# Chunk scan of a hybrid decoder step: the state product in three passes of rounded parts, and x times d on GpSimd

## The chip, the cores and the metric

The kernel runs on one core of one Trainium2 chip. A core has five engines that work at the same time, each through its own list of instructions in order: PE (TensorE, matrix products into PSUM; its weight loads, PEld, are listed apart), DVE (VectorE), ACT (ScalarE), POOL (GpSimd) and SP, which issues DMAs. An engine waits at an instruction until what it needs (data, or a buffer that is free) is there, and everything behind it waits too. The metric is the time of one execution in microseconds; a lower one is better. What is compared is the median of several executions.

## The reference

One step of a hybrid decoder layer for 512 prompt positions and 8 single new tokens (520 columns in all), model width 1024: an FFN of width 2816, a mixer, a second FFN, a final norm. The mixer adds causal pooling over windows of 2 to 16 and a Mamba-2 scan with 16 heads of 64 and a state of 128. The scan, cut to what matters:

```
xc, dtc, Bc, Cc = chunks of 128 positions; 16 heads in 2 groups of 8
Acs    = cumsum(dtc * A) within a chunk
scores = C . B                       for two positions l, s of a chunk
y_diag = sum_s scores * exp(Acs_l - Acs_s), s <= l, * dt_s * x_s
states = sum_s B_s * exp(Acs_end - Acs_s) * dt_s * x_s
h      = exp(Acs_end) * h + states   from chunk to chunk
y_off  = C_l . h * exp(Acs_l)
y      = y_diag + y_off + d_skip * x
```

All is fp32, and the kernel keeps fp32's accuracy in its products.

## The kernel before

Activations lie with their features on the 128 partitions and the 520 columns along them, in two halves of 260. A large product isn't done on fp32 operands: each operand is split in a rounded part (type fp32r, "hi", cast by ACT) and the rest ("lo", a subtraction by DVE), and three passes add hi x hi, hi x lo and lo x hi in one PSUM bank (`mm3`, lines 150 to 155, and `mm_low_last`, L157 to L165, which names the passes L160 and L165). Small products of the scan stay fp32.

The mixer is written as plans, strings of stages that are issued one after the other: the input projection's parts (x, b, z), pooling (p, c, m), the samples (s, r), the output projection (o, g, h), and for the scan A0 to A7 and B0 to B7. Stage j stands for chunk c = j mod 4 and group g = j div 4, so that a pair is named "cg": 00, 10, 20, 30, then 01, 11, 21, 31. `ssd_a` prepares a pair: PE transposes B (pb) and x (px), ACT copies B's transpose to bt, DVE masks the scores (scm) and scales x by dt (xdt), a DMA brings the sums of the decay (ab), ACT and DVE turn them into a decay matrix in place (G is ab), GpSimd makes xw (xdt times the decay to the chunk's end, we), and DVE multiplies ab by scm (L1247). `ssd_b` does the products: yo (the state hst against C, 4 matmuls of 128 columns, from chunk 1 on), pst (bt against xw, the new state's share, one matmul of 512 columns), yd (xdt against ab, 8 matmuls), then the update of hst (GpSimd multiplies by the chunk's decay cd, DVE adds pst), and on DVE E times yo, plus yd, and last X = X times d_skip + E, four operations of 128 columns with a scalar per partition (L1276). X is where x lies and where y is left; E holds exp of the sums, and the next pair's E may start once a buffer is free.

The order in which each engine gets its instructions isn't the order of the plans alone: the framework's scheduler, which places instructions by its own estimate of their times as far as the dependences allow, merges the stages of the plans, so that an edit moves work elsewhere. The banks of PSUM are 8, used in turn: a product waits until the bank that it gets has been read. xw has two buffers; ab, bt and scm have three; X is one tile.

In the names below, inx, inz and inp are banks of the input projection for x, z and pooling (the digits give the block of 128 rows and the half), zs the place to which DVE evacuates inz (L1284), PW and PU the tiles of pooling, A the accumulator of the convolution (L1025, L1027), h_60 and cb60 a sample's state and its B and C, which come back by a DMA from DRAM (L1144), catp and tlo parts of the output projection.

Of the kernel before, what the change touches and what calls it, by code (L numbers as in the profile page):

```python
# [10 lines left out]
F32 = mybir.dt.float32  # L11
F32R = mybir.dt.float32r
AF = mybir.ActivationFunctionType
ALU = mybir.AluOpType
# [3 lines left out]
P = 128  # L18
# [11 lines left out]
CH = 128  # L30
# [28 lines left out]
VEC = {}  # L59
# [838 lines left out]
def mixer(tc, ins, outs, e):  # L898
    nc = tc.nc
    cst, act, wp, tmp, dr, pool = (e[x] for x in ("cst", "act", "wp", "tmp", "dr", "pool"))  # L900
    ones, queued, squared = e["ones"], e["queued"], tuple(e["added"])
    bank, load_unit, mm3, mm_low_last, ws, v, rstd, rstds, vec, h, nx2, raw_tile, open_f2, fin, fill = (
        e[x] for x in ("bank", "load_unit", "mm3", "mm_low_last", "ws", "v", "rstd", "rstds", "vec", "h", "nx2", "raw_tile",
                       "open_f2", "fin", "fill"))
    xh, xl, _, r = nx2[0]
    xa = e["xa"][0]
    mp = pool("mx", "right")
# [16 lines left out]
    X = mp.tile([P, NX, NT], F32, tag="X", name="X")  # L924
# [279 lines left out]
    pair = {}  # L1204

    def ssd_a(c, g):
        cs = slice(c * CH, (c + 1) * CH)
        pb = bank(f"pb{c}{g}")
        nc.tensor.transpose(pb[:, :P], BC[:, g, cs], ident)
        nc.tensor.matmul(pb[:, P : 2 * P], BC[:, g, cs], BC[:, 2 + g, cs], start=True, stop=True)  # L1210
        bt = mp.tile([P, P], F32, tag="bt", bufs=3, name=f"bt{c}{g}")
        nc.scalar.copy(bt, pb[:, :P])
        scm = mp.tile([P, P], F32, tag="scm", bufs=3, name=f"scm{c}{g}")
        nc.vector.tensor_tensor(out=scm, in0=pb[:, P : 2 * P], in1=tri, op=ALU.mult)
        px = bank(f"px{c}{g}")
        for q in range(4):
            nc.tensor.transpose(px[:, q * P : (q + 1) * P], X[:, 4 * g + q, cs], ident)
        ab = mp.tile([P, 8, P], F32, tag="ab", bufs=3, name=f"ab{c}{g}")
        nc.sync.dma_start(out=ab, in_=scr_acs[c * NH + 8 * g : c * NH + 8 * g + 8].unsqueeze(0).to_broadcast([P, 8, P]))
        dtc = tok[:, 0, c, 8 * g : 8 * g + 8]  # L1220
        atc = tok[:, 1, c, 8 * g : 8 * g + 8]
        we = mp.tile([P, 8], F32, tag="we", bufs=2, name=f"we{c}{g}")
        nc.gpsimd.tensor_tensor(out=we, in0=ab[:, :, CH - 1], in1=atc, op=ALU.subtract)
        nc.scalar.activation(out=we, in_=we, func=AF.Exp)
        E = cd = None
        if c > 0:
            E = mp.tile([P, 4, P], F32, tag="E", bufs=2, name=f"E{c}{g}")
            for j in range(2):
                nc.scalar.activation(out=E[64 * j : 64 * j + 64], in_=ab[64 * j : 64 * j + 64, j::2, :], func=AF.Exp)
            cd = mp.tile([P, 8], F32, tag="cd", bufs=2, name=f"cd{c}{g}")  # L1230
            nc.scalar.activation(out=cd, in_=ab[:, :, CH - 1], func=AF.Exp)
        G = ab
        for q in range(ON_ACT):
            nc.scalar.activation(out=G[:, q], in_=ab[:, q], func=AF.Relu, scale=-1.0, bias=atc[:, q : q + 1])
        for q in range(ON_ACT, 8):
            nc.vector.tensor_scalar(out=G[:, q], in0=ab[:, q], scalar1=atc[:, q : q + 1], scalar2=0.0,
                                    op0=ALU.subtract, op1=ALU.min)
        with queued(*(held["silu"] if (c, g) == (3, 0) else ())):
            nc.scalar.activation(out=G[:, :ON_ACT], in_=G[:, :ON_ACT], func=AF.Exp, scale=-1.0)
            held["exp"] = nc.scalar.activation(out=G[:, ON_ACT:], in_=G[:, ON_ACT:], func=AF.Exp)  # L1240
        xdt = mp.tile([P, 8, 64], F32, tag="xdt", bufs=2, name=f"xdt{c}{g}")
        nc.vector.tensor_tensor(out=xdt, in0=px.rearrange("p (a b) -> p a b", a=8),
                                in1=dtc.unsqueeze(2).to_broadcast([P, 8, 64]), op=ALU.mult)
        xw = mp.tile([P, 8, 64], F32, tag="xw", bufs=2, name=f"xw{c}{g}")
        nc.gpsimd.tensor_tensor(out=xw, in0=xdt, in1=we.unsqueeze(2).to_broadcast([P, 8, 64]), op=ALU.mult)
        with queued(*(held["catp"] if (c, g) == (0, 0) else ())):
            nc.vector.tensor_tensor(out=G, in0=G, in1=scm.unsqueeze(1).to_broadcast([P, 8, P]), op=ALU.mult)  # L1247
        pair[c, g] = bt, xdt, xw, G, E, cd

    def ssd_b(c, g):  # L1250
        cs = slice(c * CH, (c + 1) * CH)
        bt, xdt, xw, G, E, cd = pair[c, g]
        if c > 0:
            yo = bank(f"yo{c}{g}")
            for q in range(4):
                nc.tensor.matmul(yo[:, q * P : (q + 1) * P], hst[:, g, q * P : (q + 1) * P], BC[:, 2 + g, cs],
                                 start=True, stop=True)
        pst = bank(f"pst{c}{g}")
        nc.tensor.matmul(pst, bt, xw.rearrange("p a b -> p (a b)"), start=True, stop=True)
        yd = bank(f"yd{c}{g}")  # L1260
        for q in range(8):
            nc.tensor.matmul(yd[64 * (q % 2) : 64 * (q % 2) + 64, (q // 2) * P : (q // 2 + 1) * P], xdt[:, q],
                             G[:, q], start=True, stop=True)
        if c == 0:
            nc.scalar.copy(hst[:, g], pst)
        else:
            hv8 = hst[:, g].rearrange("p (a b) -> p a b", a=8)
            nc.gpsimd.tensor_tensor(out=hv8, in0=hv8, in1=cd.unsqueeze(2).to_broadcast([P, 8, 64]), op=ALU.mult)
            nc.vector.tensor_tensor(out=hst[:, g], in0=pst, in1=hst[:, g], op=ALU.add)
        yr = yd.rearrange("p (q l) -> p q l", q=4)  # L1270
        if c > 0:
            nc.vector.tensor_tensor(out=E, in0=yo.rearrange("p (q l) -> p q l", q=4), in1=E, op=ALU.mult)
            nc.vector.tensor_tensor(out=E, in0=yr, in1=E, op=ALU.add)
            yr = E
        for q in range(4):
            nc.vector.scalar_tensor_tensor(out=X[:, 4 * g + q, cs], in0=X[:, 4 * g + q, cs],  # L1276
                                           scalar=v("d_skip", 4 * g + q), in1=yr[:, q], op0=ALU.mult, op1=ALU.add)

    def zproj(j):
        if not zbox:  # L1280
# [75 lines left out]
    def outs_a():  # L1356
# [16 lines left out]
        "s": samples,  # L1373
        "r": lambda n: samples(n, True),
        "A": lambda j: ssd_a(*ssd(j)),
        "B": lambda j: ssd_b(*ssd(j)),
        "z": zproj,
        "o": lambda j: wout(catp, 0, j),
# [107 lines left out]
```

## Time and profile before

| what | us |
|---|---|
| median of 3 runs (lowest, highest) | 954.37 (954.22, 955.53) |
| span of the profiled execution | 951.9 |
| PE busy | 942.5 |
| PEld (weight loads, beside PE) | 925.9 |
| DVE busy | 852.7 |
| ACT busy | 635.7 |
| POOL busy | 148.3 |

The profiled execution is known by its span, from its first instruction to its last; the time of a run has some 2.5 us more around that, by the median. The scan of the chunks lies between about 410 and 560 us. A row of a group gives the line, the engine, the operation, out<-in by the program's names, the count, and the shortest, median and longest duration in ns; a row of the timeline gives the start, the time until the group's end, the engine and the line, and in brackets how long the engine had been idle before it and for whom. Matmuls and DVE instructions overlap with the next of their queue by a little, so the time from start to start is what one costs in a row of them.

### The profile page before, as it was taken

Reading aid. Unit: us, or ns where it says so; the run is one execution under the profiler, and the core shown is the slowest. Engines: PE = TensorE matmul, PEld = TensorE weight load, DVE = VectorE, ACT = ScalarE, POOL = GpSimd, SP = SyncE. Lnnn points to the kernel's source line nnn. Section 1 sums busy time; section 2 is a strip of 40 time slices with the busy share of each in tenths; the row PEclk is TensorE's granted clock in tenths of the full one; section 3 lists DMA queues with packets and bytes.
Section 4 is the critical chain, followed back from the end, with each engine's and each line's share of the span. In section 5 each row is a group of like instructions: output and inputs, shape, how many; then the busy total and the mean of one; then the engine's idle time right before and its main releaser. Section 6 shows DMA issues by size and latency. Waiting matters only on the chain.

```text
span 951.9 us, 19681 instructions
## 1 busy us (share of the span) xinstructions
PE 942.5 (99%) x7674; PEld 925.9 (97%) x7674; DVE 852.7 (90%) x1462; ACT 635.7 (67%) x1179; POOL 148.3 (16%) x230
## 2 busy tenths in 40 slices
PE   9999999999999999999999999999999999999996
PEld 8999999999999999999999999999999999999996
DVE  6899899998988688789998998999999999999886
ACT  7777756677566455485668735777776676766774
POOL 0011100100100000046251100111112101122120
PEclk9999999999999999999999999999999999999998
DMA  7666554455553343354264453556666655776552
GB/s 205 187 166 150 143 151 135 115 140 156 134 155 95 86 134 122 92 180 138 91 184 133 141 114 115 138 122 160 163 173 176 163 146 144 171 194 185 145 180 91
DMA packets 53995, 138.35 MB, mean 145 GB/s; under 512 B 7750, under 2 KB 15878, under 8 KB 53902
## 3 DMA queue, kind: packets, MB, share of 16 engines
q1 hardware_dynamic: 39918, 104.19, 34.2%
q0 software_dynamic: 13712, 32.78, 18.7%
q8 instruction: 60, 0.98, 0.4%
q14 instruction: 33, 0.27, 0.1%
q10 hardware_dynamic: 272, 0.13, 0.0%
HBM read 129.74 MB, written 7.34 MB: 144 GB/s over the span
## 4 chain that ended last, share of the span: by engine, by line
PE 44%; DVE 2%; issue 1%; POOL 1%; DMA 1%; ACT 1%; DVEq 0%; ACTq 0%; POOLq 0%
PE A L160 8%; PE BE L160 6%; PE wo L160 5%; PE A L165 4%; PE BE L165 3%; PE wo L165 2%; PE P L311 1%; PE dh L155 1%; PE dh L151 1%; PE dh L154 1%; POOL zs L1068 1%; PE inz L151 1%; PE inz L154 1%; PE inz L155 1%; DMA room<-in_state_ssm 1%
## 5 line engine op out<-in xcount | busy, mean ns | idle before, releaser
L504 ACT COPY ac<-A 128x260 f32<-128x260 f32 x85 | 31.6, 372 | 35.4 <-PE A L155 17.3
L433 DVE TENSOR_TENSOR s<-raw 128x1024 f32<-128x1024 f32 x39 | 47.6, 1222 | 4.4 <-DMA raw<-in_w2gu 2.8
L504 ACT COPY ac<-BE 128x260 f32<-128x260 f32 x41 | 15.4, 376 | 33.6 <-PE BE L165 17.7
L151 PE MATMUL inx<-xh_mx,whi_inx 128*128 128x260 f32 x112 | 31.8, 284 | 0.0
L154 PE MATMUL inx<-xl_mx,whi_inx 128*128 128x260 f32 x112 | 31.6, 282 | 0.0
L155 PE MATMUL inx<-xh_mx,wlo_inx 128*128 128x260 f32 x112 | 31.6, 282 | 0.0
L1027 DVE SCALAR_TENSOR_TENSOR A<-U,h,A 128x544 f32<-128x544 f32 x36 | 29.0, 807 | 1.6 <-ACT A L1025 1.2
L311 PE MATMUL P<-x,raw 128*128 128x260 f32 x128 | 28.9, 385 | 0.2 <-DMA raw<-in_w1gu 0.2
L311 PEld LDWEIGHTS P<-x,raw 128*128 128x128 f32 x128 | 24.4, 192 | 4.2 <-DMA raw<-in_w1gu 0.6
L160 PE MATMUL wo<-catg,whi_wo 128*128 128x260 f32 x192 | 27.4, 285 | 0.0
L1193 ACT ACTIVATE so<-br,sxdt 128x128 f32<-128x128 f32 x64 | 22.8, 376 | 5.8 <-DVE room L1195 5.2
L160 PEld LDWEIGHTS wo<-catg,whi_wo 128*128 128x128 f32 x192 | 24.8, 188 | 0.2
L139 ACT CAST thi<-raw 128x1024 fp32r<-128x1024 f32 (+1 forms) x14 | 14.2, 1012 | 15.7 <-PE wo L160 4.8
L1304 DVE TENSOR_TENSOR h<-wo,h 128x260 f32<-128x260 f32 x48 | 19.2, 422 | 5.0 <-PE wo L165 4.7
L252 DVE TENSOR_TENSOR gs<-gq,gs 128x780 fp32r<-128x780 f32 (+1 forms) x28 | 23.3, 831 | 0.0
L151 PE MATMUL inz<-xh_mx,whi_inz 128*128 128x260 f32 x80 | 23.0, 287 | 0.0
L154 PE MATMUL inz<-xl_mx,whi_inz 128*128 128x260 f32 x80 | 22.7, 284 | 0.0
L155 PE MATMUL inz<-xh_mx,wlo_inz 128*128 128x260 f32 x80 | 22.6, 283 | 0.0
L251 ACT CAST gs<-gq 128x780 fp32r<-128x780 f32 (+1 forms) x28 | 20.6, 735 | 1.2 <-DVE gq L555 0.8
L151 PEld LDWEIGHTS inx<-xh_mx,whi_inx 128*128 128x128 f32 x112 | 21.1, 188 | 0.2 <-issue 0.2
L160 PE MATMUL A<-xth_f,qs 128*128 128x260 f32 x84 | 21.2, 283 | 0.0
L160 PE MATMUL A<-xtl_f,qs 128*128 128x260 f32 x84 | 21.2, 284 | 0.0
(3140 smaller groups left out, 4382.9 us busy)
## 6 DMA issues: line engine op xcount, KB each, us to landing
raw<-in_w2gu SPq DMA_DIRECT2D x44, 512.0 KB, 4.4
raw<-in_w1gu SPq DMA_DIRECT2D x41, 512.0 KB, 4.3
raw<-in_w_in SPq DMA_DIRECT2D x24, 512.0 KB, 3.7
raw<-in_w1d SPq DMA_DIRECT2D x16, 512.0 KB, 4.6
raw<-in_w2d SPq DMA_DIRECT2D x16, 512.0 KB, 4.6
raw<-in_w_out SPq DMA_DIRECT2D x12, 512.0 KB, 3.5
ab<-scr_acs SPq DMA_DIRECT2D x8, 512.0 KB, 5.5
h<-in_state_ssm SPq DMA_DIRECT2D x16, 256.0 KB, 3.7
```

Of the source, the lines that this page charges most:

```text
L151: first = nc.tensor.matmul(ps, whi, xhi, start=start, stop=False, **kw)
L154: nc.tensor.matmul(ps, whi, xlo, start=False, stop=False, **kw)
L155: nc.tensor.matmul(ps, wlo, xhi, start=False, stop=stop, **kw)
L160: mm = nc.tensor.matmul(ps, w, x, start=start, stop=False, **kw)
L165: nc.tensor.matmul(ps, w, xhi[k], start=False, stop=k == len(wlo) - 1, **kw)
L251: cast = nc.scalar.copy(hi, s)
L252: low = nc.vector.tensor_tensor(out=lo, in0=s, in1=hi.bitcast(F32), op=ALU.subtract)
L311: mm = nc.tensor.matmul(self.banks[f, u][b][:, :HB], ws(self.raw[f][:, u], j + 4 * q), xg[:, slot[q]], start=j == q == 0, stop=j == 3 and ...
L433: nc.vector.tensor_tensor(out=s1, in0=diag, in1=up0, op=ALU.add)
L504: self.copied = nc.scalar.copy(keep, out[:, :HB]).ins
L1027: nc.vector.scalar_tensor_tensor(out=A[:, :n], in0=U[:, j : j + n], scalar=w(j), in1=A[:, :n], op0=ALU.mult, op1=ALU.add)
L1193: nc.scalar.activation(out=o[:, q], in_=br, func=AF.Copy, scale=sxdt[:, j, b : b + 1]))
```

## The change

The state product pst isn't a matmul of fp32 operands any more. ACT rounds B's transpose to bt (fp32r, as a copy with a cast) and DVE makes the rest, btl; xw is split in xwh (ACT) and xwl (DVE); pst is `mm3` over them, three passes of 512 columns, and it is issued after yd, where it stood before yd. xw itself is made at the start of `ssd_b` instead of in `ssd_a`, by GpSimd as before; xw, xwh and xwl have one buffer each. And X = X times d + E is taken apart: GpSimd multiplies X by d_skip in place, 4 x 128 columns in one instruction, in `ssd_a` behind xdt; DVE adds E (for chunk 0, yd) to it in one instruction of 512 columns in place of four.

```diff
@@ -1208,8 +1208,9 @@
         pb = bank(f"pb{c}{g}")
         nc.tensor.transpose(pb[:, :P], BC[:, g, cs], ident)
         nc.tensor.matmul(pb[:, P : 2 * P], BC[:, g, cs], BC[:, 2 + g, cs], start=True, stop=True)
-        bt = mp.tile([P, P], F32, tag="bt", bufs=3, name=f"bt{c}{g}")
-        nc.scalar.copy(bt, pb[:, :P])
+        bt = tuple(mp.tile([P, P], F32R, tag=t, bufs=n, name=f"{t}{c}{g}") for t, n in (("bt", 3), ("btl", 2)))
+        nc.scalar.copy(bt[0], pb[:, :P])
+        nc.vector.tensor_tensor(out=bt[1], in0=pb[:, :P], in1=bt[0].bitcast(F32), op=ALU.subtract)
         scm = mp.tile([P, P], F32, tag="scm", bufs=3, name=f"scm{c}{g}")
         nc.vector.tensor_tensor(out=scm, in0=pb[:, P : 2 * P], in1=tri, op=ALU.mult)
         px = bank(f"px{c}{g}")
@@ -1241,26 +1242,33 @@
         xdt = mp.tile([P, 8, 64], F32, tag="xdt", bufs=2, name=f"xdt{c}{g}")
         nc.vector.tensor_tensor(out=xdt, in0=px.rearrange("p (a b) -> p a b", a=8),
                                 in1=dtc.unsqueeze(2).to_broadcast([P, 8, 64]), op=ALU.mult)
-        xw = mp.tile([P, 8, 64], F32, tag="xw", bufs=2, name=f"xw{c}{g}")
-        nc.gpsimd.tensor_tensor(out=xw, in0=xdt, in1=we.unsqueeze(2).to_broadcast([P, 8, 64]), op=ALU.mult)
+        skip = vec[:, VEC["d_skip"] + 4 * g : VEC["d_skip"] + 4 * g + 4].unsqueeze(2).to_broadcast([P, 4, CH])
+        xs = X[:, 4 * g : 4 * g + 4, cs]
+        nc.gpsimd.tensor_tensor(out=xs, in0=xs, in1=skip, op=ALU.mult)
         with queued(*(held["catp"] if (c, g) == (0, 0) else ())):
             nc.vector.tensor_tensor(out=G, in0=G, in1=scm.unsqueeze(1).to_broadcast([P, 8, P]), op=ALU.mult)
-        pair[c, g] = bt, xdt, xw, G, E, cd
+        pair[c, g] = bt, xdt, we, G, E, cd
 
     def ssd_b(c, g):
         cs = slice(c * CH, (c + 1) * CH)
-        bt, xdt, xw, G, E, cd = pair[c, g]
+        bt, xdt, we, G, E, cd = pair[c, g]
+        xw = mp.tile([P, 8, 64], F32, tag="xw", name=f"xw{c}{g}")
+        nc.gpsimd.tensor_tensor(out=xw, in0=xdt, in1=we.unsqueeze(2).to_broadcast([P, 8, 64]), op=ALU.mult)
+        xwh, xwl = (mp.tile([P, 512], F32R, tag=t, name=f"{t}{c}{g}") for t in ("xwh", "xwl"))
+        xw = xw.rearrange("p a b -> p (a b)")
+        nc.scalar.copy(xwh, xw)
+        nc.vector.tensor_tensor(out=xwl, in0=xw, in1=xwh.bitcast(F32), op=ALU.subtract)
         if c > 0:
             yo = bank(f"yo{c}{g}")
             for q in range(4):
                 nc.tensor.matmul(yo[:, q * P : (q + 1) * P], hst[:, g, q * P : (q + 1) * P], BC[:, 2 + g, cs],
                                  start=True, stop=True)
-        pst = bank(f"pst{c}{g}")
-        nc.tensor.matmul(pst, bt, xw.rearrange("p a b -> p (a b)"), start=True, stop=True)
         yd = bank(f"yd{c}{g}")
         for q in range(8):
             nc.tensor.matmul(yd[64 * (q % 2) : 64 * (q % 2) + 64, (q // 2) * P : (q // 2 + 1) * P], xdt[:, q],
                              G[:, q], start=True, stop=True)
+        pst = bank(f"pst{c}{g}")
+        mm3(pst, *bt, xwh, xwl, True, True)
         if c == 0:
             nc.scalar.copy(hst[:, g], pst)
         else:
@@ -1272,9 +1280,8 @@
             nc.vector.tensor_tensor(out=E, in0=yo.rearrange("p (q l) -> p q l", q=4), in1=E, op=ALU.mult)
             nc.vector.tensor_tensor(out=E, in0=yr, in1=E, op=ALU.add)
             yr = E
-        for q in range(4):
-            nc.vector.scalar_tensor_tensor(out=X[:, 4 * g + q, cs], in0=X[:, 4 * g + q, cs],
-                                           scalar=v("d_skip", 4 * g + q), in1=yr[:, q], op0=ALU.mult, op1=ALU.add)
+        xs = X[:, 4 * g : 4 * g + 4, cs]
+        nc.vector.tensor_tensor(out=xs, in0=yr, in1=xs, op=ALU.add)
 
     def zproj(j):
         if not zbox:
```

The order of the instructions changes with it. Three places follow. First DVE around the decay matrix of pair 30 (its product with the mask is the row `ab30<-ab30,scm30`); E20 and xdt01 belong to the pairs 20 and 01, zs<-inz10 evacuates a bank of z, sxdt belongs to the samples. Before:

```order
L1284 TENSOR_TENSOR zs_5724<-inz01_5729,r_mx_3921 128x260
L1273 TENSOR_TENSOR E20_5556<-yd20_5787,E20_5556 128x512
L1247 TENSOR_TENSOR ab30_5695<-ab30_5695,scm30_5688 128x1024
L1214 TENSOR_TENSOR scm01_5809<-pb01_5804,tri_4294 128x128
L1242 TENSOR_TENSOR xdt01_5831<-px01_5811,tok_4361 128x512
L1276 SCALAR_TENSOR_TENSOR X_4306<-X_4306,h_69,E20_5556 128x128 x4
L1284 TENSOR_TENSOR zs_5724<-inz10_5841,r_mx_3921 128x260
L1247 TENSOR_TENSOR ab01_5816<-ab01_5816,scm01_5809 128x1024
```

After:

```order
L1281 TENSOR_TENSOR E20_5565<-yd20_5805,E20_5565 128x512
L1260 TENSOR_TENSOR xwl30_5916<-xw30_5913,xwh30_5915 128x512
L1213 TENSOR_TENSOR btl01_5827<-pb01_5823,bt01_5826 128x128
L1215 TENSOR_TENSOR scm01_5830<-pb01_5823,tri_4294 128x128
L1135 TENSOR_TENSOR sxdt_4369<-sdt_4367,X_4306 128x32
L1291 TENSOR_TENSOR zs_5738<-inz00_5742,r_mx_3921 128x260
L1291 TENSOR_TENSOR zs_5738<-inz01_5743,r_mx_3921 128x260
L1284 TENSOR_TENSOR X_4306<-E20_5565,X_4306 128x4x128
L1291 TENSOR_TENSOR zs_5738<-inz10_5861,r_mx_3921 128x260
L1249 TENSOR_TENSOR ab30_5710<-ab30_5710,scm30_5703 128x1024
L1249 TENSOR_TENSOR ab01_5837<-ab01_5837,scm01_5830 128x1024
```

The product for ab30 stood right behind yd20's addition; now xwl30, btl01, scm01, three evacuations of z and the addition to X of pair 20 stand between, and xdt01 comes after it.

Second, pair 10: PE's products, and GpSimd ahead of them. PE before:

```order
L1217 MATMUL px20_5546<-ident_4292,X_4306 128x128 x4
L1256 MATMUL yo10_5576<-BC_4307,hst_4374 128x128 x4
L1259 MATMUL pst10_5581<-xw10_5460,bt10_5429 128x512
L1262 MATMUL yd10_5583<-ab10_5438,xdt10_5458 64x128 x8
L151 MATMUL inx70_5605<-xh_mx_3918,whi_inx7_5601 128x260
L154 MATMUL inx70_5605<-xl_mx_3919,whi_inx7_5601 128x260
```

PE after:

```order
L1218 MATMUL px20_5555<-ident_4292,X_4306 128x128 x4
L1264 MATMUL yo10_5590<-BC_4307,hst_4374 128x128 x4
L1268 MATMUL yd10_5595<-ab10_5446,xdt10_5466 64x128 x8
L151 MATMUL pst10_5604<-xwh10_5586,bt10_5435 128x512
L151 MATMUL inx70_5618<-xh_mx_3918,whi_inx7_5614 128x260
L154 MATMUL inx70_5618<-xl_mx_3919,whi_inx7_5614 128x260
L155 MATMUL inx70_5618<-xh_mx_3918,wlo_inx7_5615 128x260
L154 MATMUL pst10_5604<-xwl10_5587,bt10_5435 128x512
L155 MATMUL pst10_5604<-xwh10_5586,btl10_5436 128x512
```

yd10 stands ahead of pst10, and three passes of the projection inx70 stand between the first pass of pst10 and the other two. GpSimd, where PW2 and PU2 are pooling's, before:

```order
L1068 TENSOR_TENSOR PW2_1_5404<-PU2_5398 128x654
L1075 COPY spool_4302<-PU2_5398 128x120
L1068 TENSOR_TENSOR PW2_2_5406<-PW2_1_5404 128x652
L1245 TENSOR_TENSOR xw10_5460<-xdt10_5458,we10_5440 128x512
L1068 TENSOR_TENSOR PW2_4_5408<-PW2_2_5406 128x648
```

GpSimd after (the row with X is pair 10's multiplication by d_skip; d_skip lies in h's tile):

```order
L1068 TENSOR_TENSOR PW2_1_5410<-PU2_5404 128x654
L1075 COPY spool_4302<-PU2_5404 128x120
L1247 TENSOR_TENSOR X_4306<-X_4306,h_69 128x4x128
L1068 TENSOR_TENSOR PW2_2_5412<-PW2_1_5410 128x652
L1256 TENSOR_TENSOR xw10_5584<-xdt10_5466,we10_5448 128x512
L1068 TENSOR_TENSOR PW2_4_5414<-PW2_2_5412 128x648
```

The multiplication of X by d is put between the copy of pooling's state and the second sum of pooling, and xw10 now stands behind both.

Third, DVE where z is evacuated beside the samples (h_50 to h_70 are samples' states). Before:

```order
L1144 TENSOR_TENSOR h0_40_6182<-h0_40_6182,cb40_6180 128x512
L1144 TENSOR_TENSOR h0_50_6191<-h0_50_6191,cb50_6189 128x512
L1284 TENSOR_TENSOR zs_5724<-inz40_6221,r_mx_3921 128x260
L1144 TENSOR_TENSOR h0_60_6200<-h0_60_6200,cb60_6198 128x512
L1284 TENSOR_TENSOR zs_5724<-inz41_6222,r_mx_3921 128x260
L1144 TENSOR_TENSOR h0_70_6209<-h0_70_6209,cb70_6207 128x512
L141 TENSOR_TENSOR wlo_inz7_6568<-raw_74,whi_inz7_6567 128x1024
```

After:

```order
L1144 TENSOR_TENSOR h0_50_6222<-h0_50_6222,cb50_6220 128x512
L1291 TENSOR_TENSOR zs_5738<-inz40_6252,r_mx_3921 128x260
L1260 TENSOR_TENSOR xwl11_6319<-xw11_6316,xwh11_6318 128x512
L1291 TENSOR_TENSOR zs_5738<-inz41_6253,r_mx_3921 128x260
L1144 TENSOR_TENSOR h0_60_6231<-h0_60_6231,cb60_6229 128x512
L1144 TENSOR_TENSOR h0_70_6240<-h0_70_6240,cb70_6238 128x512
L141 TENSOR_TENSOR wlo_inz7_6606<-raw_74,whi_inz7_6605 128x1024
```

The evacuation of inz41 and the subtraction xwl11 stand ahead of the sample's product with cb60; the evacuation stood behind it.

## The prediction

> **What bounds the kernel.** I read the page's busy times first, then the busy times by stretches of 10 us through the mixer, then the chain of waits there, the groups of the tiles that the change touches, and the timeline at the places where TensorE (PE) comes close to waiting. The first lines say what the kernel is made of:
>
> ```profile
> span 951.9 us, 19681 instructions
> PE 942.5 (99%) x7674; PEld 925.9 (97%) x7674; DVE 852.7 (90%) x1462; ACT 635.7 (67%) x1179; POOL 148.3 (16%) x230
> ```
>
> PE is busy for 99% of the span, so time is won only by shorter work on PE or by removing a wait of PE, and lost by any new wait. The median of the runs, 954.37, lies 2.5 us above this span; I make the sum on the trace and add it to the median. About 0.2% (1.9 us) is what a measurement of this kernel can tell from no change: faster is below 952.46, slower above 956.28.
>
> The stretches that hold the chunk scan:
>
> ```profile
> 440.00:450.00 10.00, 10.00 (x88) 9.07 (x87) 9.55 (x17) 4.26 (x8) 10.00 (x15) 1.00 0.30 88
> 450.00:460.00 10.00, 10.00 (x86) 10.00 (x86) 10.00 (x24) 6.69 (x14) 2.73 (x5) 1.00 0.23 88
> 460.00:470.00 10.00, 10.00 (x88) 9.07 (x87) 9.01 (x17) 7.22 (x17) 2.27 (x5) 1.00 0.51 162
> 500.00:510.00 10.00, 9.69 (x83) 8.52 (x82) 7.08 (x14) 7.54 (x35) 1.66 (x2) 1.00 0.48 141
> ```
>
> After the stretch come PE, weight loads, DVE, ACT and GpSimd (POOL), then the granted clock, 1.00 throughout. Of all stretches from 400 to 570 only 500–510 has PE idle, 0.31 us. The others are full, but DVE is full or nearly full beside it, and GpSimd is full in 440–450. So PE's waits are not there because DVE is in time, by how much is the question.
>
> **PE: the state product.** The chain of waits gives the steps from one product to the next for pair 21:
>
> ```profile
> 522.79 0.89 PE yo L1256 x8
> 523.68 0.86 PE pst L1259 x2
> 524.54 1.02 PE yd L1262 x16
> ```
>
> The fp32 product of 512 columns is two records and takes 0.86 of PE. What a pass of rounded parts costs at 512 columns no row shows. The nearest rows are passes of 260 columns, one every 0.12 us, and what follows a change from fp32 work (yd) to rounded work:
>
> ```profile
> 448.17 0.39 PE L151 MATMUL inx<-xh_mx,whi_inx 128*128 128x260 f32 x1
> 448.39 0.28 PE L154 MATMUL inx<-xl_mx,whi_inx 128*128 128x260 f32 x1
> 448.51 0.28 PE L155 MATMUL inx<-xh_mx,wlo_inx 128*128 128x260 f32 x1
> 448.63 0.28 PE L151 MATMUL inx<-xh_mx,whi_inx 128*128 128x260 f32 x1
> ```
>
> By columns, 0.12 x 512/260 = 0.236, three passes 0.71, a saving of 0.15 a pair. If a pass instead takes half of one fp32 record (0.43/2 = 0.215), it is 0.645 and 0.215. The first pass after yd takes 0.22 rather than 0.12; yd is followed by rounded work now too, so this 0.10 moves and is not added, except where fp32 transposes follow pst. Taking 0.17, nearer to the measured 260-column step, eight pairs save 1.36 us (1.2 to 1.7).
>
> The Trainium skill, page "FP8 and Floating Point Precision", section "TensorE Precision Notes", says that a true fp32 product makes four passes through the array. By it three of four passes remain, 0.215 a pair, and the sum below would be 0.36 lower, 953.5; the step of 0.12 at 260 columns speaks for a little less.
>
> **What is put on the other engines.** Per pair, from these groups and from the starts in the DVE timeline further down:
>
> ```profile
> L1276 DVE SCALAR_TENSOR_TENSOR X<-X,h,E x24: 337/344/1156, 454.9 to 547.2; 128x128 f32<-128x128 f32 x24
> L1265 ACT COPY hst<-pst x2: 587/587/587, 430.5 to 486.2; 128x512 f32<-128x512 f32 x2
> L1245 POOL TENSOR_TENSOR xw<-xdt,we x8: 1039/1094/1892, 416.6 to 522.2; 128x512 f32<-128x512 f32 x8
> L1247 DVE TENSOR_TENSOR ab<-ab,scm x8: 1207/1215/2062, 423.2 to 525.1; 128x1024 f32<-128x1024 f32 x8
> ```
>
> GpSimd gets x times d, priced like xw (the same 512 columns): 1.04 a pair, 8.3 in all. ACT gets the rounded copy xwh, like the copy of pst: 0.59 a pair; the rounding of bt takes the place of a copy. DVE loses four operations that start 1.04 apart as a group (454.88 to 455.92 below) and gets the 512-column addition (0.60, E's step), xwl (0.60) and btl (0.20, scm's step): +0.36 a pair, 2.9 in all. None of it lies on PE; it counts where PE arrives soon after.
>
> **Pair 30, the largest loss.** PE's yd30 needs ab30, the last DVE step of its decay matrix. Before:
>
> ```profile
> 454.88 1.13 DVE L1276 SCALAR_TENSOR_TENSOR X<-X,h,E 128x128 f32<-128x128 f32 x4
> 455.92 0.78 DVE L1027 SCALAR_TENSOR_TENSOR A<-U,h,A 128x544 f32<-128x544 f32 x1
> 461.62 3.24 DVE L1027 SCALAR_TENSOR_TENSOR A<-U,h,A 128x544 f32<-128x544 f32 x3 [0.92 <-ACT A L1025]
> 467.88 0.68 DVE L1273 TENSOR_TENSOR E<-yd,E 128x512 f32<-128x512 f32 x1
> 468.48 1.22 DVE L1247 TENSOR_TENSOR ab<-ab,scm 128x1024 f32<-128x1024 f32 x1
> 469.61 0.29 DVE L1214 TENSOR_TENSOR scm<-pb,tri 128x128 f32<-128x128 f32 x1
> 469.81 0.69 DVE L1242 TENSOR_TENSOR xdt<-px,tok 128x512 f32<-128x512 f32 x1
> 470.41 2.72 DVE L1276 SCALAR_TENSOR_TENSOR X<-X,h,E 128x128 f32<-128x128 f32 x4
> 473.05 0.42 DVE L1284 TENSOR_TENSOR zs<-inz,r_mx 128x260 f32<-128x260 f32 x1
> 473.39 1.21 DVE L1247 TENSOR_TENSOR ab<-ab,scm 128x1024 f32<-128x1024 f32 x1
> ```
>
> ```profile
> 471.63 1.02 PE L1259 MATMUL pst<-xw,bt 128*128 128x512 f32 x2
> 472.58 0.33 PE L1262 MATMUL yd<-ab,xdt 128*64 128x128 f32 x2
> ```
>
> ab30 ends at 469.70, yd30 starts at 472.58: 2.88 to spare. After, ab30 stands behind more (the first piece of order above): xwl10, xwl20, xwl30 (3 x 0.60), btl20, btl30, btl01 (3 x 0.20), and moved ahead of it scm01 (0.20), the addition of pair 20 (0.60) and zs of inz10 (0.34), less 0.44 for pair 10's shorter addition: +3.1. Of this DVE's one wait, 0.92 for ACT at 460.70, gives some back, but ACT itself is later by xwh20's 0.59, so what comes after that wait decides: 0.59 + 0.60 + 0.20 + 0.20 + 0.60 + 0.34 = 2.5. ab30 then ends at 472.2. PE reaches yd30 earlier than before, because yd now stands ahead of pst and three pairs have gained: 471.63 - 3 x 0.17 = 471.1. PE waits 1.1 us. The bounds: 0, if the moved steps fall into time in which DVE would have waited; 2.7, if the 0.92 is not given back (472.8) and one GpSimd operation holds ab30 up for 1.04. I take 1.1, the sum without collision.
>
> **Pair 10.** GpSimd was continuously busy, and now x times d of pair 10 stands ahead of xw10 (the third piece of order):
>
> ```profile
> 440.62 1.27 POOL L1068 TENSOR_TENSOR PW<-PW 128x652 f32<-128x652 f32 x1
> 441.85 1.04 POOL L1245 TENSOR_TENSOR xw<-xdt,we 128x512 f32<-128x512 f32 x1
> 446.19 1.02 PE L1259 MATMUL pst<-xw,bt 128*128 128x512 f32 x2
> 447.14 1.09 PE L1262 MATMUL yd<-ab,xdt 128*64 128x128 f32 x16
> ```
>
> xw10 ended at 442.89, 3.3 before pst10. It now ends 1.04 later, 443.9 (up to 445.2 if the operations around it wait for DVE), then xwh10 (0.59) and xwl10 (0.60) on queues that hold other work: 445.9 to 447.5. The pass that reads xwl10 would start 0.22 after pst10's first, at about 447.2 (yd10 is ahead of it now), and three passes of inx70 are put between (0.36), which covers most of the rest. I take +0.2 (0 to 1.0). For pair 11 the same sum leaves no wait, within some tenths.
>
> **The wait at 504.** The one idle time of PE in the scan is made by DVE:
>
> ```profile
> 503.35 0.69 DVE L1144 TENSOR_TENSOR h<-h,cb 128x512 f32<-128x512 f32 x1 [2.92 <-DMA cb<-scr_bc]
> 503.96 0.42 DVE L1284 TENSOR_TENSOR zs<-inz,r_mx 128x260 f32<-128x260 f32 x1
> 504.44 0.39 PE L151 MATMUL inz<-xh_mx,thi 128*128 128x260 f32 x1 [0.31 <-DVE zs L1284]
> ```
>
> inz50 needs the bank that zs of inz41 empties, and that evacuation stands behind a product which waits for a DMA. In the new order it stands ahead of that product, so this wait goes: -0.4 (the idle 0.31 and the start of the pipeline; bounds 0 and 0.5). SP's order changes by three loads and stores that trade places; none is waited for by PE before 500, so I cost that at nothing, covered by the 2.9 us in which DVE, not PE, waits for cb.
>
> **Sum.** -1.36 - 0.4 + 1.1 + 0.2 = -0.46: 954.37 - 0.46 = 953.9, no change that could be measured. Its own range is 953.0 to 955.3.
>
> **Rivals.** *A, the whole gain.* No new wait at pairs 30 and 10: 954.37 - 1.76 = 952.6, 952.2 with the cheaper passes. For it: 2.88 and 3.3 us to spare before. Against: the 2.5 us just counted on an engine that is busy 9 to 10 of 10.
>
> *B, slower: GpSimd and DVE hold each other up.* The maxima in the groups above (xw 1.89 against 1.04, ab times scm 2.06 against 1.21, an addition 1.16 against 0.34) and the group at 470.41 (2.72 for what took 1.13 at 454.88, while xw of pair 01 ran on GpSimd) show that operations of the two that read from SBUF come out longer together by about what one of them takes. The change adds eight such operations on GpSimd and eight on DVE (xwl). At pair 30 each collision ahead of ab30 costs 1.04, since the slack is gone: x times d of pair 30, the update of hst for pair 30 (which starts with yo30, just as ab30 runs) and xw30 give 1.1 + 3 x 1.04 = 4.2 in place of 1.1: 957.0. It decides from the third collision on (two make 956.0), or from two there and one at pair 11.
>
> The Trainium skill, page "SBUF — State Buffer", section "Who interferes with whom", states that a DVE instruction with two SBUF inputs contends with a GpSimd instruction that reads SBUF, whoever starts first keeping the port for the whole instruction. This case's trace agrees (2.72 against 1.13); by that rule B is likelier than chance meetings make it, since both new DVE steps have two SBUF inputs for c > 0.
>
> *C, the passes save nothing.* If a 512-column pass cost 0.287 (a third of 0.86), the gain of 1.36 goes and the waits stay: 955.3. The step of 0.12 at 260 columns speaks against it.
>
> **Chances.** The forecast 0.46, A 0.20, B 0.22, C 0.12. Faster by over 0.2%: 0.12 of A (its lower half and a little more) and 0.04 of the forecast, 0.16. Slower: 0.20 of B, 0.06 of the forecast's upper end, 0.04 of C: 0.30. Within: 0.54. The range runs from A with the cheaper passes, 952.2, to B's price with a little beyond, 957.3.
>
> **What the next profile would show.** The three passes of pst at steps of 0.22 to 0.24; idle time of PE's weight loads before yd30 near 471, released by DVE's ab, of about 1 us; no idle PE near 504; x times d at 1.04 and, if B holds, many at 2 and ab times scm at 2 as well. I am wrong if ab30 ends before yd30's place (then A), or if PE's sum of idle time in 400–570 exceeds 3 us (then B).

## The result and the profile after

The changed kernel takes 958.99 us (median; 957.12 to 962.75), the kernel before 954.50 beside it: 1.0050 times as long, 95% interval 1.0036 to 1.0063. Forecast was 953.9, range 952.2 to 957.3. The profiled execution is the shortest of the six, 957.12, with a span of 955.4, 3.5 us above that of before.

The first lines of its page, and the stretches of the scan (columns as before):

```profile
span 955.4 us, 19693 instructions
PE 942.4 (99%) x7682; PEld 929.1 (97%) x7682; DVE 859.0 (90%) x1454; ACT 640.7 (67%) x1187; POOL 159.5 (17%) x238
```

```profile
450.00:460.00 10.00, 9.60 (x81) 9.39 (x80) 10.00 (x19) 5.59 (x13) 5.04 (x6) 1.00 0.21 66
460.00:470.00 10.00, 9.46 (x83) 8.71 (x82) 10.00 (x20) 7.80 (x18) 3.80 (x5) 1.00 0.42 128
470.00:480.00 10.00, 7.64 (x69) 7.18 (x69) 10.00 (x19) 7.99 (x15) 3.46 (x5) 1.00 0.28 100
500.00:510.00 10.00, 10.00 (x89) 9.53 (x89) 8.69 (x14) 9.72 (x35) 4.29 (x4) 1.00 0.44 116
```

PE's idle time at 504 is gone, and 3.3 us of idle time stand between 450 and 480, where there was none; DVE is full there. The waits of PE from 440 to 600 (us in total, times, longest):

```profile
PE yd L1268 <- DVE ab L1249: 2.4, 1, 2.4
PE px L1218 <- DVE catp L1093: 0.5, 1, 0.5
PE pm L151 <- ACT catp L1082: 0.4, 1, 0.4
```

PE's saving is there. In pair 30, from the start of pst (471.63, in the prediction) to the projection's next pass it was 1.98 us before; after, from yd on, which now comes first, 1.82:

```profile
473.61 0.39 PE L151 MATMUL inp<-xh_mx,whi_inp 128*128 128x260 f32 x1
```

```profile
475.51 1.09 PE L1268 MATMUL yd<-ab,xdt 128*64 128x128 f32 x16 [2.36 <-DVE ab L1249]
476.53 0.50 PE L151 MATMUL pst<-xwh,bt 128*128 128x512 f32 x1
476.87 0.40 PE L154 MATMUL pst<-xwl,bt 128*128 128x512 f32 x1
477.11 0.39 PE L155 MATMUL pst<-xwh,btl 128*128 128x512 f32 x1
477.33 0.28 PE L151 MATMUL inp<-xh_mx,whi_inp 128*128 128x260 f32 x1
```

That is 0.16 a pair, about 1.3 us for eight; the other seven pairs show the same to 0.01 (in pair 10 without the three passes of inx70 that stand between). What undid it is seen in the timelines of GpSimd, DVE and ACT of the changed kernel:

```profile
451.08 1.52 POOL L1256 TENSOR_TENSOR xw<-xdt,we 128x512 f32<-128x512 f32 x1
452.57 1.27 POOL L1073 TENSOR_TENSOR PW<-PW,PU 128x7 f32<-128x7 f32 x1
455.90 1.05 POOL L1247 TENSOR_TENSOR X<-X,h 128x512 f32<-128x512 f32 x1 [1.91 <-PE px L1218]
461.21 1.89 POOL L1256 TENSOR_TENSOR xw<-xdt,we 128x512 f32<-128x512 f32 x1 [0.42 <-ACT ab L1235]
471.02 1.04 POOL L1247 TENSOR_TENSOR X<-X,h 128x512 f32<-128x512 f32 x1 [0.67 <-PE px L1218]
473.23 1.05 POOL L1276 TENSOR_TENSOR hst<-hst,cd 128x512 f32<-128x512 f32 x1 [1.17 <-PE yo L1264]
```

```profile
455.58 1.65 DVE L1237 TENSOR_SCALAR ab<-ab,tok 128x128 f32<-128x128 f32 x4
462.52 2.06 DVE L1237 TENSOR_SCALAR ab<-ab,tok 128x128 f32<-128x128 f32 x4
465.19 0.87 DVE L1093 SCALAR_TENSOR_TENSOR catp<-pm,h,catp 128x260 fp32r<-128x260 f32 x2
468.41 0.77 DVE L1027 SCALAR_TENSOR_TENSOR A<-U,h,A 128x544 f32<-128x544 f32 x1
471.31 0.80 DVE L1135 TENSOR_TENSOR sxdt<-sdt,X 128x32 f32<-128x32 f32 x1
473.64 1.72 DVE L1249 TENSOR_TENSOR ab<-ab,scm 128x1024 f32<-128x1024 f32 x1
```

```profile
453.87 0.62 ACT L1082 CAST catp<-PW 128x512 fp32r<-128x512 f32 x1 [0.61 <-POOL PW L1073]
469.22 0.63 ACT L1029 ACTIVATE X<-A 128x512 f32<-128x512 f32 x1 [2.10 <-DVE A L1027]
471.27 0.63 ACT L1240 ACTIVATE ab<-ab 128x512 f32<-128x512 f32 x1
471.81 0.61 ACT L1241 ACTIVATE ab<-ab 128x512 f32<-128x512 f32 x1
```

Beside each long GpSimd operation a DVE instruction is drawn out: a group of four that takes 0.86 alone took 1.65 and 2.06, sxdt 0.80, where it took 0.18 before, and ab30 itself 1.72 instead of 1.22, beside the update of hst at 473.23. The order adds to it: E20's product with yo and the subtraction tlo (L141), 1.7 us together, now stand ahead of the convolution's last block (L1027). That block ends at 469.18 instead of 464.86, ACT's silu waits for it for 2.10 us, and the exponentials of ab30, which stand behind that silu, end at 472.42. They aren't what ab30 waits for: DVE is never idle from 445.68 on, and it comes to ab30 at 473.64, 1.2 us after them, behind the additions and evacuations that the new order puts ahead. The smaller waits are made by the same two things: pm waits for a rounding that waits for pooling on GpSimd (452.57, behind xw20, and drawn out itself), and px01 for an evacuation (465.19) behind the group of 2.06.

### The profile page after: what moved, and what is told of

It reads as the page before. It is cut to its first block, busy times and chain, and to the rows that moved or that the text cites. A ratio compares the mean times of both kernels' runs of the same rounds, so it can differ in the third digit from the quotient of the medians.

```text
span 955.4 us, 19693 instructions
## 1 busy us (share of the span) xinstructions
PE 942.4 (99%) x7682; PEld 929.1 (97%) x7682; DVE 859.0 (90%) x1454; ACT 640.7 (67%) x1187; POOL 159.5 (17%) x238
## 5 line engine op out<-in xcount | busy, mean ns | idle before, releaser
L1027 DVE SCALAR_TENSOR_TENSOR A<-U,h,A 128x544 f32<-128x544 f32 x36 | 28.0, 780 | 0.6 <-ACT A L1025 0.3
L154 PEld LDWEIGHTS inx<-xl_mx,whi_inx 128*128 128x128 f32 x112 | 21.1, 188 | 0.1
```

The lines of the kernel that those rows point to most:

```text
L154: nc.tensor.matmul(ps, whi, xlo, start=False, stop=False, **kw)
L1027: nc.vector.scalar_tensor_tensor(out=A[:, :n], in0=U[:, j : j + n], scalar=w(j), in1=A[:, :n], op0=ALU.mult, op1=ALU.add)
```

## The experiments

Each kernel was timed beside the kernel before on the same chip; the ratios and their 95% intervals are against it. In the code, `...` stands for lines left out. Three theories stood at the start or came up: G, GpSimd's multiplication holds DVE up; D, DVE's own new steps and their order do; and after the first runs H, the exponentials held behind the silu set ab30, and L, DVE's load as a whole bounds the scan, with S against it, DVE has slack and single orders alone hurt.

**The two parts apart.** The passes alone (e1) and the multiplication alone (e2). That xw is made in the second stage and has one buffer belongs to the passes in every kernel tried, and was not tried alone.

```diff
 # e1: from the changed kernel
-        nc.gpsimd.tensor_tensor(out=xs, in0=xs, in1=skip, op=ALU.mult)
...
-        nc.vector.tensor_tensor(out=xs, in0=yr, in1=xs, op=ALU.add)
+        for q in range(4):
+            nc.vector.scalar_tensor_tensor(out=X[:, 4 * g + q, cs], in0=X[:, 4 * g + q, cs],
+                                           scalar=v("d_skip", 4 * g + q), in1=yr[:, q], op0=ALU.mult, op1=ALU.add)
```

> The change without its part on x times d: the state product in three passes, xw in the second stage, but X times d + E by DVE in four operations as before. Theory G (GpSimd's multiplication of X delays DVE and its own queue, and that made the new waits of PE, 3.6 us at 454, 465 and 473): no multiplication, so PE waits at most 1 us there, saves 1.8 us in the eight products, and the time is 952.5 to 954. Theory D (the new steps on DVE, xwl and btl, and the order in which ab of pair 30 comes last, made them): the waits stay, 957 to 959, PE waits 2 us or more before yd of pair 30.

Measured 961.36 (1.0075, 1.0058 to 1.0091): above both theories. PE waits 3.6 us before yd30, and more:

```profile
PE yd L1265 <- DVE ab L1246: 3.6, 1, 3.6
PE wo L160 <- DVE h L1309: 2.0, 1, 2.0
```

The order of this kernel puts ab01, the four operations on X and three evacuations ahead of ab30; the exponentials end at 474.06 and ab30 starts at 474.17. It speaks for D, and shows something else: the stretches around that wait.

```profile
472.00:476.00 4.00, 0.57 (x6) 0.57 (x8) 4.00 (x9) 3.94 (x6) 2.19 (x2) 0.70 0.00 2
476.00:478.00 2.00, 2.00 (x16) 1.57 (x13) 2.00 (x6) 1.97 (x6) 0.23 (x1) 0.50 0.00 0
478.00:480.00 2.00, 2.00 (x9) 1.81 (x8) 2.00 (x4) 0.89 (x3) 1.73 (x1) 0.50 0.69 260
480.00:484.00 4.00, 4.00 (x34) 4.00 (x33) 2.88 (x11) 2.77 (x8) 0.85 (x1) 0.95 0.40 132
```

The granted clock falls to 0.50 during the wait and stays there for some 5 us of matmuls behind it, which costs some 2 us more. In the changed kernel's profile, with its wait of 2.4 us, it stays 1.00.

```diff
 # e2: from the kernel before
+        nc.gpsimd.tensor_tensor(out=xs, in0=xs, in1=skip, op=ALU.mult)
...
-        for q in range(4):
-            nc.vector.scalar_tensor_tensor(out=X[:, 4 * g + q, cs], in0=X[:, 4 * g + q, cs],
...
+        nc.vector.tensor_tensor(out=xs, in0=yr, in1=xs, op=ALU.add)
```

> The other part alone: fp32 state product as before the change, xw in the first stage, X times d by GpSimd and E added to it by DVE in one instruction. Theory G: PE waits 2 to 4 us in 450 to 480 without saving anything in the product: 956.5 to 958.5. Theory D: DVE has 0.44 us less a pair, nothing else waits: 953.5 to 954.8.

Measured 960.46 (1.0056, 1.0044 to 1.0068). Without any new DVE step in the product it is as slow as the whole change (the intervals overlap): G is right that the multiplication alone costs, D wrong on this kernel. But G had the waits between 450 and 480, where only 0.4 us is found, and a time below 958.5. The loss has no one place: the largest wait is 1.3 us of the output projection for a DMA, then four of 0.4 to 0.5 for DVE. That DMA is late by DVE as well: it is issued behind a step of ACT (L247) at 550.92, in the kernel before 544.89, and ACT had waited for DVE until 548.09, before until 544.25. By the starts of the same matmuls in both traces 1.9 us of the 6.9 arise only in the second FFN; no run shows why.

**The multiplication left out, or on another engine.** All three start from the changed kernel.

```diff
 # e3 drops the line; e4 gives it to DVE; e5 to ACT
-        nc.gpsimd.tensor_tensor(out=xs, in0=xs, in1=skip, op=ALU.mult)
 # e4
+        nc.vector.tensor_tensor(out=xs, in0=xs, in1=skip, op=ALU.mult)
 # e5
+        for q in range(4):
+            nc.scalar.mul(X[:, 4 * g + q, cs], X[:, 4 * g + q, cs], v("d_skip", 4 * g + q))
```

> The change with the multiplication of X by d left out (the term d times x is then x, so the output isn't the reference's); all else as changed, the addition in one instruction too. Theory G: the waits at 454, 465 and 473 shrink to 1 us in all: 952.5 to 954, and the DVE instructions beside GpSimd (sxdt 0.80, ab 1.65 and 2.06) return to 0.2 to 0.3 and 0.9. Theory D: the wait before yd of pair 30 stays over 2 us and the time over 956.5.

> The change with X times d made by DVE (one instruction of 512 columns, about 0.6 us) in place of GpSimd. Theory G: no collision, DVE has 0.6 us a pair more that is not doubled, so faster than the change: 954 to 957. Theory D: DVE is later by 0.6 us a pair, 2.4 us by pair 30, and the time is 960 to 962.

> The changed kernel with X times d made by ACT in four instructions of 128 columns (about 0.39 us each, 1.5 a pair) in place of GpSimd. Theory G (GpSimd's multiplication costs by holding DVE up): DVE's instructions are short as in the kernel without the multiplication, and the time is 956 to 957.5, 1.5 to 3 us below the changed kernel's. Theory H: ACT is later by 1.5 us a pair, the silu and the exponentials too, and the time is 959 to 961.

Without it 955.99 (1.0015, 1.0006 to 1.0024); on ACT 955.88 (1.0018, 1.0008 to 1.0027); on DVE 962.95 (1.0089, 1.0075 to 1.0104). Moved from GpSimd to ACT, where its four instructions of 0.39 us start 0.30 apart, the multiplication costs nothing that could be told from leaving it out: G's direction holds, and some 3 of the 4.5 us are its price on GpSimd in this kernel. H, which expected ACT to be late, falls. But e3 lies between G's 952.5 to 954 and D's 956.5, and on DVE it is worst, even above D's 960 to 962. Both ways of spending DVE's time count. The waits that e5 has left, all for DVE:

```profile
PE yd L1267 <- DVE ab L1248: 1.1, 1, 1.1
PE wo L160 <- DVE h L1310: 0.8, 1, 0.8
PE yo L1263 <- DVE hst L1276: 0.5, 1, 0.5
```

**The largest wait taken away.** Two edits leave PE's and GpSimd's orders as they are:

```diff
 # from the changed kernel; e6: ab30's exponentials need not follow the silu
-        with queued(*(held["silu"] if (c, g) == (3, 0) else ())):
+        with queued():
 # e7: four DVE steps put behind ab30's product (its handle is kept in held)
...
+        with queued(*((held["ab", 3, 0],) if (c, g) == (2, 0) else ())):
             nc.vector.tensor_tensor(out=xs, in0=yr, in1=xs, op=ALU.add)
...
+            with queued(*((held["ab", 3, 0],) if j < 2 else ())):
                 nc.vector.tensor_tensor(out=zbox[0][:, j, hs], in0=bs[b][:, :HB], in1=r[:, hs], op=ALU.mult)
```

> The changed kernel without the one rule that the exponentials of ab of pair 30 on ACT are issued behind the silu of the convolution's last block; PE's and GpSimd's orders are unchanged by it, ACT's and DVE's change only near there. Theory H (the wait before yd of pair 30 is long because ab30's exponentials stand behind that silu, and the silu is late because DVE, with xwl, btl and the doubled instructions, ends the convolution late): ab30 is ready before PE comes, the 2.5 us go, px of pair 01 may wait up to 0.7 for the silu, and the time is 1.5 to 2.5 us below the changed kernel's. Theory D (DVE reaches ab30 late by its own queue): ab30 is at most 0.5 us earlier and the time the same.

> The changed kernel with ab30's last step put ahead of four others on DVE (two evacuations of z for the first block, the addition to X of pair 20, one evacuation of the second block), nothing else moved. Theory H: the step can't start before the exponentials at 472.4, 1.2 us earlier than it did; PE's wait shrinks by 1.2 to 1.8 us and the time by as much. Theory D: the four steps are 2.0 us of DVE, and the wait shrinks by 2.0 or more.

> The changed kernel once more, unaltered, for what differs from one execution to the next. If the 1 us that the changed kernel lost between 650 and 750 us (the second FFN, which the change doesn't touch) is the change's own, it is there again; if it is chance of the transfers, the loss there differs by some tenths to 1 us. In 440 to 480 the waits of PE (0.6, 0.7, 2.5) are the same to 0.2 us under each theory.

Measured 960.26 and 958.67, against 958.25 for the changed kernel once more: no gain. Yet the wait is gone in e6, as H said, and 0.7 in e7. In e7 DVE comes early enough to be idle for 0.34 us and starts ab30 right behind the exponentials:

```profile
472.86 0.62 ACT L1241 ACTIVATE ab<-ab 128x512 f32<-128x512 f32 x1
```

```profile
473.51 1.22 DVE L1249 TENSOR_TENSOR ab<-ab,scm 128x1024 f32<-128x1024 f32 x1 [0.34 <-ACT ab L1241]
```

So in the changed kernel the order on DVE held ab30, and the exponentials are the next limit, some 1.2 us earlier. PE's waits in e6:

```profile
PE yo L1264 <- DVE hst L1277: 1.0, 1, 1.0
PE px L1218 <- ACT X L1029: 0.8, 1, 0.8
PE inz L151 <- DVE E L1280: 0.6, 1, 0.6
PE pst L154 <- DVE xwl L1260: 0.3, 1, 0.3
```

What was won at 473 came back at px01, then at pair 11 (pst), at 510 (inz) and at 535 (yo31): PE had merely reached DVE sooner (the waits for catp, 0.5 and 0.4, are there as in the changed kernel; from 440 to 600 the sum is 3.6 in e6 and 3.2 in e7, against 3.3). This made theory L. The repeat has the three waits of the scan to the tenth. By the starts of the same matmuls in both traces the first profile lost another 1.0 us against before from 564 to the end, in the second FFN, and the repeat nothing, so that part of the first span was chance; but it has one wait more, at 425, which the first hadn't, for a part of pooling that DVE makes (e6 and e7 have it too, 0.9 and 1.1):

```profile
PE pm L154 <- DVE catp L1083: 1.1, 1, 1.1
```

**DVE's load priced by itself.** One DVE instruction more a pair in the kernel before, PE's and GpSimd's orders but for one step each as they were, while DVE's own order moves with it; and the kernel before with less:

```diff
 # e12: from the kernel before
+        more = mp.tile([P, 8, 64], F32R, tag="more", name=f"more{c}{g}")
+        nc.vector.tensor_tensor(out=more, in0=xw, in1=xdt, op=ALU.subtract)
 # e11: from the kernel before, fp32 product kept
+        for q in range(4):
+            nc.scalar.mul(X[:, 4 * g + q, cs], X[:, 4 * g + q, cs], v("d_skip", 4 * g + q))
-        for q in range(4):
-            nc.vector.scalar_tensor_tensor(out=X[:, 4 * g + q, cs], in0=X[:, 4 * g + q, cs],
...
+        nc.vector.tensor_tensor(out=xs, in0=yr, in1=xs, op=ALU.add)
```

> The kernel before with one DVE instruction more a pair (a subtraction of 512 columns with both inputs in SBUF into a tile that nothing reads, the size of xwl); the orders of PE and GpSimd stay as before. Theory L (DVE's load bounds the scan: it had 6.5 us to spare between 440 and 545, and the change used it up): 4.8 us more of DVE turn into waits of PE of 2 to 4 us, and the time is 956 to 959. Theory S (DVE has slack, only GpSimd's multiplication and single orders hurt): within 0.5 us of before.

> The kernel before (fp32 state product) with X times d made by ACT in four instructions and E added by DVE in one: DVE has 0.44 us less a pair, GpSimd the same, ACT 1.5 us more. Theory L: DVE gains 3.5 us of room, no new wait, and since PE had only one short wait the time is 953.5 to 954.8; so the passes of rounded parts cost 1 to 2 us net against it (955.9 with them). Theory S: the passes are a gain, so this kernel without them is slower than the one with them, 956.5 or more.

> The changed kernel with X times d on ACT and, besides, ab30's last step ahead of two evacuations of z, the addition to X of pair 20 and one evacuation more. Theory L: PE's wait before yd of pair 30 (1.1 us) shrinks, but what it gains comes back as waits at pair 11 or 31, so the time is within 0.7 us of the same kernel without it, 955.2 to 956.6. Theory S: the 1.1 us stay won, 954.3 to 955.0.

The unused subtraction makes it 961.75 (1.0072, 1.0060 to 1.0084), even more than L expected; its waits are those of the changed kernel, the same ab30 first:

```profile
PE yd L1264 <- DVE ab L1247: 1.9, 1, 1.9
PE px L1217 <- ACT X L1029: 1.0, 1, 1.0
PE yo L1258 <- DVE hst L1271: 1.0, 1, 1.0
PE psr_y L210 <- DVE X L1331: 0.9, 1, 0.9
```

Part of it is order: ab30 stands behind ab01 there too. And of the 8.6 us by which its profiled execution is longer than that of before, 2.8 arise in the second FFN, by the starts of the same matmuls. With less on DVE, e11, PE has no wait at all from 440 to 600, and the time is that of before: 954.63 against 954.88 (1.0001, 0.9991 to 1.0011). e10, which is e5 with e7's order, is 956.03 (1.0015, 1.0006 to 1.0023): its wait for ab30 is 0.6 instead of 1.1, and 0.4 came up at pst11, as L expected. The busy times from 440 to 545 in before, the changed kernel, e12, e11, e1 and e3, in this order:

```profile
sum 105.00, PE 104.69 PEld 97.83 DVE 98.54 ACT 72.16 POOL 37.38; mean PE 104.69 PEld 97.83 DVE 98.54 ACT 72.16 POOL 37.38
```

```profile
sum 105.00, PE 101.70 PEld 97.90 DVE 102.10 ACT 75.66 POOL 46.48; mean PE 101.70 PEld 97.90 DVE 102.10 ACT 75.66 POOL 46.48
```

```profile
sum 105.00, PE 99.84 PEld 91.90 DVE 99.82 ACT 70.73 POOL 36.52; mean PE 99.84 PEld 91.90 DVE 99.82 ACT 70.73 POOL 36.52
```

```profile
sum 105.00, PE 105.00 PEld 98.29 DVE 95.91 ACT 81.13 POOL 38.83; mean PE 105.00 PEld 98.29 DVE 95.91 ACT 81.13 POOL 38.83
```

```profile
sum 105.00, PE 101.14 PEld 97.19 DVE 97.28 ACT 77.11 POOL 42.15; mean PE 101.14 PEld 97.19 DVE 97.28 ACT 77.11 POOL 42.15
```

```profile
sum 105.00, PE 103.51 PEld 99.47 DVE 103.56 ACT 77.80 POOL 36.78; mean PE 103.51 PEld 99.47 DVE 103.56 ACT 77.80 POOL 36.78
```

DVE has 6.5 us to spare before, and the first four kernels would fit a rule that whoever exceeds that load waits. The last two refute it: e1, with a smaller busy time than before, is among the slowest, and e3, the fullest, loses 1.4 us. Where PE waits, the stretch holds less work, and a drawn-out step counts as busy, so these sums don't measure a load. What does rank the kernels is the time that an edit's own steps add to DVE, by their durations alone (xwl 0.60, btl 0.20, the addition to X 0.60 in place of 1.04, a multiplication 0.60), beside what the kernel loses by its ratio:

| kernel | added to DVE, us | time against before, us |
|---|---|---|
| e11 | -3.5 | +0.1 |
| e3, e5, e10 | +2.9 | +1.4, +1.7, +1.4 |
| e12 | +4.8 | +6.9 |
| e1 | +6.4 | +7.2 |
| e4 | +7.7 | +8.5 |
| with X times d on GpSimd: e2 | -3.5 | +5.3 |
| the changed kernel, e6, e7 | +2.9 | +4.8, +5.5, +4.6 |

Those with +2.9, e1 and e4 have PE's saving of 1.3 in them. So L is borne out in this form: more work on DVE costs about its own length or somewhat more, and the multiplication on GpSimd costs as well. It stays open how much of each loss is the load and how much the order, since no run added load with DVE's order held. No kernel tried beats the one before.

By the ratios the account is: the passes with X times d on ACT against the fp32 product with X times d on ACT, 1.0018 - 1.0001, +1.6 us; GpSimd in place of ACT, 1.0050 - 1.0018, +3.1 us. The two prices don't simply add: with the fp32 product, GpSimd in place of ACT costs 1.0056 - 1.0001, +5.2 us, and the passes then cost nothing more (1.0050 against 1.0056).

## Why the prediction was wrong

- **The state product, -1.36.** Right: 0.16 a pair, 1.3 us; passes at steps of 0.24 and 0.22 behind a first one of 0.34, as the columns and the 0.10 of the change to rounded work said.
- **The wait at 504, -0.4.** Right in the changed kernel's profile. Another wait came up near there (inz, 0.6 and 0.3) in e6 and e7, whose PE arrives earlier.
- **Pair 30, +1.1.** The step that failed. The place, the engine and the releaser were right, and 2.4 lies inside the bounds given; what was wrong is the choice of "the sum without collision". ab30 was to end at 472.2 and ended at 475.36. DVE took it up 5.2 us later than before (473.64 instead of 468.48), with no idle time on the way from 445.68. Set side by side step for step, the two traces give for this: new and moved steps +3.3 (I had 3.1, without btl10), less idle time -0.7 (I had -0.6), and some +2.4 by DVE steps drawn out beside GpSimd, which I had put at nothing; the last of them, ab30 itself, adds 0.5. That the wait is 2.4 and not more is partly luck: PE came at 473.15, not at 471.1, half of it by the two waits at 454 and 465. ACT's exponentials, which the prediction left out, were done at 472.42 and did not set this time, but would have been next (e7).
- **Pair 10, +0.2.** pst10 itself did not wait. The wait came 7 us further, at pm, for pooling's last step behind xw20 on the same queue, and at px01: 0.9 together, in no term. I had followed xw on GpSimd's queue but not what stands behind it.
- **What no term held.** Single waits were added up as if DVE caught up between them. It doesn't: e6 and e7 remove or shorten the largest wait and win nothing. Of the 5.0 us by which the difference of the medians (+4.5) misses the forecast (-0.46), pair 30 is 1.3, the waits at pm and px01 0.7, the second FFN in the profiled execution 1.0, and 1.0 is that the median stands further above the span than before (3.6 against 2.6); the remaining 1.0 is in pieces of 0.1 to 0.4 that I haven't followed.
- **Rivals.** B was the case that came, by its mechanism and its sign of being wrong (3.3 us of idle time, above 3); its chance, 0.22, was too low. All three collisions that it named are there: x times d at 455.90, xw30 at 461.21 and the update of hst at 473.23. That its price of 957.0 lies beside the profiled 957.12 is luck: it had 4.2 us of wait at pair 30, where 2.4 came, and the difference was made up by waits elsewhere and by the 1.0 us of the second FFN. A and C are refuted by the waits and by the measured passes. The page "SBUF — State Buffer" of the Trainium skill, section "Who interferes with whom", was the better guide: it lets a DVE instruction of the `tensor_scalar` kind contend as well, and here groups of those were among the most stretched (1.65 and 2.06 for 0.86).
- **The median above the profile.** Of the twelve executions of the changed kernel with its repeat, eight had a mean granted clock of 0.993 to 0.995 and took 957.9 to 962.8 us, four had 0.996 or 0.997 and took 957.1 to 957.7; before, e6 and e7 have 0.996 to 0.998 in each. e1's trace shows how a longer wait halves the clock; that the wait at 473 (with the one at 425 ahead of it or not) does so in those executions is a conclusion from the clocks, since the two profiled ones show 1.00 there. The four stand about 1.7 us above e5's 955.88, so that some 1.4 of the 3.1 us between GpSimd and ACT would go with the lower clock, which e5 (0.996 or 0.997 in each) doesn't have.

## What to carry to other kernels

Before an engine gets "hidden" work, add up its idle time over the whole stretch and not its slack at single waits. DVE had 6.5 us idle in 105 here; steps of 2.9 us more cost 2.7 to 3.0 us, beside the 1.3 that PE saved, and repairing the largest wait only moved it. Price such work with its collisions: the multiplication on GpSimd beside a nearly full DVE cost 3.1 to 5.2 us, while ACT, at 72 of 105 us, took it at no cost that could be measured. And follow a delayed step through its own queue to what stands behind it (here pooling behind xw20), and into the next engine's queue (here a silu, and the exponentials held behind it). Busy time in a fixed stretch doesn't rank kernels whose main engine waits in it.

## What the runs showed of the hardware

A wait of PE of 2.4 us left the granted clock at 1.00 in two traces. In e1, with a wait of 3.6 us (from 471.9 to 475.4), it fell to 0.50 some 1.7 us into the wait (0.70 from 472 to 476 makes 2.4 us at 0.50) and stayed there for 5 us of matmuls. In e4, with 3.5 us (to 477.4), it fell only at the end of the wait (0.84 from 476 to 478) and stayed for some 3.3 us. Matmuls of yd took 421 ns at 0.50 instead of 272:

```profile
L1265 PE MATMUL yd<-ab,xdt x16: 421/421/473, 475.4 to 477.0; 128*64 128x128 f32 x16
```

The Trainium skill's page "TensorE: Matmul & The Clock Gate", section "Part 1: The HAM clock gate (the "warmup" mystery)", has the clock halve after an idle window of about 3.4 us; the waits of 2.4 us and of 3.5 and 3.6 lie on either side of it, but in e1 the clock fell sooner after PE's last work, at 1.7 us. So in these traces waits of 3.5 and 3.6 us have a price beyond their length and those of 2.4 don't. The length alone doesn't say when the clock falls; and the changed kernel's executions at a lower clock suggest, without a trace, that a wait of about 2.4 us can have that price too.
